# A fused transformer layer on one core: the closing norm of a mixture of experts, split into all tokens and the tokens of the last two experts

## The chip, the core and the metric

The kernel runs on one core of a Trainium2 chip. The metric is the device time of the whole kernel in microseconds (us). The engines are named as in the profile: PE is TensorE's matmuls, PEld its weight loads, DVE is VectorE, ACT is ScalarE, POOL is GpSimd, SP is SyncE; a q behind a name is the sequencer, which issues DMAs.

## The reference

One layer on 512 tokens of width 1024, in float32: a mixer of two attentions, then a mixture of experts, each followed by a residual and a LayerNorm. The change touches the end of the second half alone, so only that is shown.

```python
def layer_norm(x, g, b):
    xf = x.astype(jnp.float32)
    mu = jnp.mean(xf, axis=-1, keepdims=True)
    var = jnp.mean(jnp.square(xf - mu), axis=-1, keepdims=True)
    return ((xf - mu) * lax.rsqrt(var + LN_EPS)).astype(x.dtype) * g + b

# grouped_top2_moe: 16 experts, each token takes 2 of them
    for e in range(N_EXPERTS):
        hdn = jax.nn.silu(x2d @ w_gate[e]) * (x2d @ w_up[e])
        out = out + combine[:, e:e + 1] * (hdn @ w_down[e])

# reference
        ffn = grouped_top2_moe(x, w_router, b_router, w_gate[l], w_up[l], w_down[l])
        x = layer_norm(ALPHA * x + ffn, ln2_g[l], ln2_b[l])
```

## The kernel before

The experts are computed one after the other. An expert's tokens are gathered into slots (128 slots, or 64 from expert 10 on, `SMALL`); the token number of each slot stands in `idx`. The weights come as 512 KB loads, issued by SP in the order of use into a large ring of buffers (`big()`, `prefetch`), as early as a buffer is free. Experts from the fourth on are taken in the order of their token counts, so that 14 and 15, the last two, have the fewest tokens.

Each expert makes two products: gate and up (`pg`, eight steps c, from the lines under `if few:`), then, after `silu`, a transpose (`hidden_small`) and the second product (`down_small`, in `pu`). The second product of expert e - 1 stands inside expert e's steps, at c == 4 (`AHEAD`). Up to expert 13, POOL adds the result to the rows of `x1d` in DRAM, which holds the residual stream, by an indirect DMA (`scatter`).

The last two experts have no scatter. Their results stay on the chip: the 64 slots of expert 14 are put in partitions 0 to 63 and those of expert 15 in 64 to 127 of one pair of tiles (`split_y`: high and low parts). `final_loads`, at c == 3 of expert 15, loads the four 128-token tiles of `x1d` (`base`). A matrix `sel` of zeros and ones says which slot belongs to which token; `combine` multiplies it with the results on TensorE, so that each of the four tiles of tokens gets its sums, which DVE adds to `base` (`norm_add`). Then come mean, squares, power and the two closing multiplications, in 512-wide halves spread over DVE, ACT and POOL in an order that is written out by hand, and eight stores of 128 x 512 to the output.

In this part of the kernel every instruction goes through `ko`, which keeps the written order on each engine; an engine takes its instructions in that order and waits at the first that isn't ready. Two groups of `busy` matmuls (`WARM3`, `WARM4`) stand around the last transpose.

## Time and profile before

| | |
|---|---|
| median of 3 runs | 701.64 us (701.2 to 702.09) |
| the profiled execution's own time | 701.37 us |
| its span, first to last instruction | 699.6 us |
| busy: PE, PEld, DVE, ACT, POOL | 95%, 70%, 62%, 51%, 17% of the span |
| granted TensorE clock, mean | 0.989 |
| DMA | 155.35 MB, mean 222 GB/s |

Busy time is that of instructions of the program; a matmul's end is modelled, so that a busy PE isn't PE at its peak. The granted clock is a share of 2.4 GHz. A DMA share of 1.00 means that all 16 DMA engines of the core were taken. The idle time in brackets is that of the engine just before the instruction, with what ended it.

### The profile page before, as it was taken

The page shows a single profiled execution, that of the slowest core. Times are in us where ns is not written, and L with a number is a line of the kernel's source. Part 1 is how long each engine was busy: PE and PEld are TensorE (multiplying, and loading weights), DVE is VectorE, ACT ScalarE, POOL GpSimd, SP SyncE. Part 2 cuts the span into 40 slices and gives each one's busy share as a digit, 9 for nine tenths or more (in the row PEclk, how much of TensorE's full clock was granted, in tenths as well). Part 3 has the DMA queues.
Part 4 walks back from the last instruction along what each step waited for, and adds up shares of the span by engine and source line. Part 5 has one row for each costly group of instructions (what it writes and reads, how often), then busy time and mean ns, then how long its engine had stood idle before and what let it go on. Part 6 is the DMA issues. An engine that isn't in the chain of part 4 may idle for free.

```text
span 699.6 us, 9694 instructions
## 1 busy us (share of the span) xinstructions
PE 664.3 (95%) x3254; PEld 488.9 (70%) x3254; DVE 436.8 (62%) x740; ACT 354.0 (51%) x574; POOL 119.4 (17%) x189
## 2 busy tenths in 40 slices
PE   8999999999999999999999888999999999999970
PEld 5888778777787678888888766888888886533220
DVE  5343666667767337252545999999999998222246
ACT  5433585786656424232221236888888886211133
POOL 2000333232332110000000010111111112112016
PEclk9999999999999999999999999999999999999995
DMA  7422222211211193226993859999999999999953
GB/s 287 164 91 90 91 94 87 67 56 60 77 45 61 60 322 104 90 91 232 363 364 121 309 198 339 357 383 379 368 365 372 336 351 371 323 339 353 384 216 120
DMA packets 47062, 155.35 MB, mean 222 GB/s; under 512 B 7471, under 2 KB 7471, under 8 KB 47010
## 3 DMA queue, kind: packets, MB, share of 16 engines
q1 hardware_dynamic: 40848, 142.62, 55.8%
q0 software_dynamic: 3536, 7.82, 4.6%
q10 hardware_dynamic: 2626, 4.27, 1.8%
q8 instruction: 26, 0.43, 0.3%
q14 instruction: 26, 0.21, 0.1%
HBM read 146.87 MB, written 12.58 MB: 228 GB/s over the span
## 4 chain that ended last, share of the span: by engine, by line
PE 77%; DMA 7%; DVE 6%; issue 3%; ACT 3%; POOL 2%; DVEq 0%; POOLq 0%; SPq 0%; ACTq 0%
PE pj L149 6%; PE pj L150 5%; PE pj L151 5%; DMA raw<-in_wu_dram 5%; PE a L150 4%; PE a L151 4%; PE a L149 4%; PE py L149 3%; PE py L151 3%; PE py L150 3%; PE pg L149 2%; PE pg L1214 2%; PE pu L151 2%; PE pg L151 2%; PE pu L150 2%
## 5 line engine op out<-in xcount | busy, mean ns | idle before, releaser
L131 DVE TENSOR_TENSOR wlo<-raw,whi 128x1024 fp32r<-128x1024 f32 x169 | 202.4, 1222 | 109.2 <-ACT whi L124 105.3
L124 ACT ACTIVATE whi<-raw 128x1024 fp32r<-128x1024 f32 x169 | 174.7, 1057 | 103.8 <-issue 27.0
L149 PE MATMUL pj<-xhi,whi 128*128 128x512 f32 x192 | 81.8, 426 | 0.0
L151 PE MATMUL pj<-xhi,wlo 128*128 128x512 f32 x192 | 75.8, 395 | 0.0
L150 PE MATMUL pj<-xlo,whi 128*128 128x512 f32 x192 | 75.6, 394 | 0.0
L1041 POOL DMA_INDIRECT x1d<-y,idx x14 | 21.6, 1545 | 148.2 <-ACT y L1036 76.4
L1214 PE MATMUL pg<-raw,gh 128*64 128x512 f32 x192 | 46.1, 599 | 0.6 <-DMA raw<-in_wu_dram 0.4
L151 PEld LDWEIGHTS pj<-xhi,wlo 128*128 128x128 f32 x192 | 36.1, 188 | 8.5
L149 PEld LDWEIGHTS pj<-xhi,whi 128*128 128x128 f32 x192 | 36.6, 191 | 4.3 <-issue 0.2
L150 PEld LDWEIGHTS pj<-xlo,whi 128*128 128x128 f32 x192 | 36.4, 190 | 4.2
L312 POOL TENSOR_TENSOR p<-bt,g 128x127 f32<-128x127 f32 (+3 forms) x32 | 25.7, 812 | 52.6 <-DVE g L309 40.1
L298 POOL TENSOR_SCALAR p<-p,st 128x128 f32<-128x128 f32 (+3 forms) x32 | 17.1, 535 | 97.5 <-DVE st L297 97.5
L149 PE MATMUL py<-whi,hh 128*128 128x512 f32 x80 | 33.1, 414 | 0.0
L151 PE MATMUL py<-whi,hl 128*128 128x512 f32 x80 | 31.5, 394 | 0.0
L150 PE MATMUL py<-wlo,hh 128*128 128x512 f32 x80 | 31.5, 394 | 0.0
L309 DVE TENSOR_TENSOR_SCAN g<-l 128x128 f32<-128x128 f32 (+3 forms) x32 | 26.1, 834 | 8.4 <-ACT l L305 6.0
L1214 PEld LDWEIGHTS pg<-raw,gh 128*64 128x64 f32 x192 | 14.2, 136 | 23.7 <-issue 19.8
L893 POOL DMA_INDIRECT xg<-x1k,idx x15 | 20.5, 1370 | 58.6 <-PE pg L151 20.0
L149 PE MATMUL pg<-whi,gh 128*128 128x512 f32 x72 | 30.2, 420 | 0.0
L151 PE MATMUL pu<-whi,gl 128*128 128x512 f32 x72 | 28.5, 396 | 0.0
L151 PE MATMUL pg<-whi,gl 128*128 128x512 f32 x72 | 28.4, 395 | 0.0
L150 PE MATMUL pu<-wlo,gh 128*128 128x512 f32 x72 | 28.4, 394 | 0.0
(290 smaller groups left out, 1415.1 us busy)
## 6 DMA issues: line engine op xcount, KB each, us to landing
raw<-in_wd_dram SPq DMA_DIRECT2D x64, 512.0 KB
raw<-in_wg_dram SPq DMA_DIRECT2D x63, 512.0 KB
raw<-in_wu_dram SPq DMA_DIRECT2D x63, 512.0 KB
raw<-in_wq_dram SPq DMA_DIRECT2D x32, 512.0 KB
raw<-in_wout_dram SPq DMA_DIRECT2D x8, 512.0 KB
raw<-in_wv_dram SPq DMA_DIRECT2D x7, 512.0 KB
bt<-in_relr_dram SPq DMA_DIRECT2D x8, 256.0 KB
raw<-in_wupa_dram SPq DMA_DIRECT2D x4, 512.0 KB
```

Of the source, the lines that this page charges most:

```text
L124: ko(nc.scalar.activation(hi, raw, AF.Copy))
L131: ko(e.tensor_tensor(lo, raw, hi.bitcast(F32), op=OP.subtract))
L149: ko(nc.tensor.matmul(o, ahi, bhi, start=start, stop=False))
L150: ko(nc.tensor.matmul(o, ahi, blo, start=False, stop=False))
L151: ko(nc.tensor.matmul(o, alo, bhi, start=False, stop=stop))
L298: nc.gpsimd.tensor_scalar(p[:, :n], p[:, :n], st[:, 2, i:i + 1], 1.0, op0=OP.mult, op1=OP.mult)
L309: nc.vector.tensor_tensor_scan(g[:, :n][:, ::-1], kp[:, :n][:, ::-1], kp[:, :n][:, ::-1], 1.0, op0=OP.mult, op1=OP.bypass)
L312: nc.gpsimd.tensor_tensor(p[:, :n - 1], bt[:, :n - 1], g[:, 1:n], op=OP.mult)
L893: ko(nc.gpsimd.indirect_dma_start(out=xgb[e % NXG][:m], out_offset=None, in_=x1k, in_offset=bass.IndirectOffsetOnAxis(ap=idx[:m, e:e + 1], ...
L1041: ko(nc.gpsimd.indirect_dma_start(out=x1d, out_offset=bass.IndirectOffsetOnAxis(ap=idx[:m, e:e + 1], axis=0), in_=y[:m], in_offset=None, b ...
L1214: ko(nc.tensor.matmul(pgu[0][o], xgt[e][:, kt], w[:, ws], start=kt == 0, stop=kt == KT - 1))
```

## The change

All four tiles of tokens are normed as they stand in `x1d` without the last two experts. For the tokens that do have a slot with expert 14 or 15 this is not the result; these are normed a second time by slot, and their rows are written over the first ones.

- `final_loads` takes six loads in the order base 0, base 1, gain, base 2, base 3, offset, into buffers of another ring (`spare`); the gain and offset rows of the norm were loaded after the last product before.
- `pair_rows` gathers by indirect DMA the `x1d` rows of the 128 slots of experts 14 and 15 (`ids`).
- `same_tokens` makes a 128 x 128 matrix that is 1 where two slots hold the same token, by one matmul of ones with a diagonal of the token numbers. A token may have a slot with both experts; `same` adds up its two results in both slots.
- `copy_last` copies the two results into `ylast`, once, in plain fp32. TensorE forms pair rows plus `same` times `ylast` in `pz`.
- Tiles 0 and 1 have their statistics from DVE (`stats_v`), tiles 2 and 3 from ACT (`sum_a`, `square_a`).
- Tile 0 is finished by DVE. For tiles 1, 2 and 3 TensorE makes the output: the identity times the offset row (`offset_pe`) plus a diagonal of the inverse deviations times the centred and gained tile (`finish_pe`), both in fp32; ACT copies it out.
- The pair rows are normed by DVE from `pz`, and an indirect DMA of POOL writes them to the output.

```diff
-    off4 = const.tile([P, NT], F32, name="off4")
-    nc.gpsimd.iota(off4, pattern=[[-P, NT]], base=1, channel_multiplier=0,
...
-    def split_y(e, py, hf, part):
-        ws = slice(hf * 512, (hf + 1) * 512)
-        es = slice(0, HS) if e == NE - 2 else slice(HS, P)
-        o = py[hf * HS:(hf + 1) * HS]
-        if part == 0:
-            ko(nc.scalar.activation(yhl[0][es, ws], o, AF.Copy))
-            return
-        ko(nc.vector.tensor_tensor(yhl[1][es, ws], o, yhl[0][es, ws].bitcast(F32), op=OP.subtract))
...
-    def final_select():
-        sel = big(F32R)[:, :S]
-        gid = ep.tile([P, NT + 1], F32, name="gid")
-        ko(nc.vector.tensor_copy(gid[:HS, NT:], idx[:HS, NE - 2:NE - 1]))
-        ko(nc.vector.tensor_copy(gid[HS:, NT:], idx[HS:, NE - 1:]))
-        ko(nc.vector.tensor_scalar(gid[:, :NT], off4, gid[:, NT:], None, op0=OP.add))
-        for i in range(NT):
-            ko(nc.vector.tensor_scalar(sel[:, i * P:(i + 1) * P], slots, gid[:, i:i + 1], None, op0=OP.is_equal))
-        return sel
+    def spare(name, dt=F32):
+        return ring.tile([P, D], dt, name=name, bufs=RING)
...
+    halves = [slice(0, 512), slice(512, D)]
     def final_loads():
-        for i in range(NT):
-            base.append(big())
-            nc.sync.dma_start(base[i], x1d[i * P:(i + 1) * P])
-        lnw2.extend(big() for _ in range(2))
+        base.extend(spare(("whi", "wlo")[i // 2]) for i in range(NT))
+        lnw2.extend(spare("whi") for _ in range(2))
+        for k in (0, 1, "g", 2, 3, "b"):
+            if k in ("g", "b"):
+                t, src = (lnw2[0], ln2g) if k == "g" else (lnw2[1], ln2b)
+                ko(nc.sync.dma_start(t, src.to_broadcast([P, D])))
+            else:
+                ko(nc.sync.dma_start(base[k], x1d[k * P:(k + 1) * P]))
+    def pair_rows():
+        ids = pair["ids"] = ep.tile([P, 1], I32, name="ids")
+        ko(nc.vector.tensor_copy(ids[:HS], idx[:HS, NE - 2:NE - 1]))
+        ko(nc.vector.tensor_copy(ids[HS:], idx[HS:, NE - 1:]))
+        so = pair["sum"] = big()
+        ko(nc.gpsimd.indirect_dma_start(
+            out=so, out_offset=None, in_=x1d, in_offset=bass.IndirectOffsetOnAxis(ap=ids, axis=0),
+            bounds_check=S - 1, oob_is_err=False))
+    def same_tokens():
+        gid = ep.tile([P, 1], F32, name="gid")
+        ko(nc.vector.tensor_copy(gid, pair["ids"]))
+        diag = spare("wlo")[:, :P]
+        ko(nc.vector.tensor_scalar(diag, ident, gid, None, op0=OP.mult))
+        rows = eps_.tile([P, P], F32, name="py0")
+        onesf = ep.tile([P, 512], F32, name="gl0")[:, :P]
+        nc.gpsimd.memset(onesf, 1.0)
+        ko(nc.tensor.matmul(rows, onesf, diag, start=True, stop=True))
+        same = spare("wlo")[:, :P]
+        ko(nc.vector.tensor_scalar(same, rows, gid, None, op0=OP.is_equal))
+        return same
+    def copy_last(e, py):
+        es = slice(0, HS) if e == NE - 2 else slice(HS, P)
+        ko(nc.scalar.activation(ylast[es, :512], py[:HS], AF.Copy))
+        ko(nc.vector.tensor_copy(ylast[es, 512:], py[HS:]))
...
-                    yhl.extend(big(F32R) for _ in range(2))
-                    for hf in range(2):
-                        for part in range(2):
-                            split_y(e - 1, py, hf, part)
+                    ylast = big()
+                    copy_last(e - 1, py)
...
-            if last and c == 1:
-                sel = final_select()
...
+                pair_rows()
+                same = same_tokens()
...
+    def stats_v(i, src):
+        st = ep.tile([P, 2, 6], F32, name="st")
+        for hf in range(2):
+            ko(nc.vector.bn_stats(st[:, hf], src[hf]))
+        ko(nc.vector.bn_aggr(mv[:, i, 0:2], st.rearrange("p a b -> p (a b)")))
+    def dev_v(i):
+        ko(nc.gpsimd.tensor_scalar(mv[:, i, 1:2], mv[:, i, 1:2], EPS / ALPHA ** 2, 1.0, op0=OP.add, op1=OP.mult))
+        ko(nc.gpsimd.tensor_tensor(mv[:, i, 2:3], mv[:, i, 1:2], mhalf, op=OP.pow))
+    def sum_a(i):
+        ko(nc.scalar.activation(junk, base[i], AF.Copy, accum_out=mv[:, i, 3:4]))
+        ko(nc.gpsimd.tensor_scalar(mv[:, i, 4:5], mv[:, i, 3:4], -1.0 / D, 1.0, op0=OP.mult, op1=OP.mult))
+        ko(nc.gpsimd.tensor_scalar(mv[:, i, 0:1], mv[:, i, 3:4], 1.0 / D, 1.0, op0=OP.mult, op1=OP.mult))
+    def square_a(i):
+        ko(nc.scalar.activation(junk, base[i], AF.Square, bias=mv[:, i, 4:5], accum_out=mv[:, i, 5:6]))
+        ko(nc.gpsimd.tensor_scalar(mv[:, i, 1:2], mv[:, i, 5:6], 1.0 / D, EPS / ALPHA ** 2, op0=OP.mult, op1=OP.add))
+        ko(nc.gpsimd.tensor_tensor(mv[:, i, 2:3], mv[:, i, 1:2], mhalf, op=OP.pow))
+    def gain(i, o, src, w=slice(0, D)):
+        ko(nc.vector.scalar_tensor_tensor(o, src, mv[:, i, 0:1], lnw2[0][:, w], op0=OP.subtract, op1=OP.mult))
+    def diag_dev(i):
+        ko(nc.vector.tensor_scalar(dg[:, i * P:(i + 1) * P], ident, mv[:, i, 2:3], None, op0=OP.mult))
+    po2 = {}
+    def offset_pe(i):
+        for hf in range(2):
+            name = {1: ("pg", "pg"), 2: ("th", "tx"), 3: ("pu", "pu")}[i][hf]
+            po2[i, hf] = eps_.tile([P, 512], F32, name=name, **({"bufs": 2} if name in ("pg", "pu") else {}))
+            ko(nc.tensor.matmul(po2[i, hf], ident, lnw2[1][:, halves[hf]], start=True, stop=False))
+    def finish_pe(i):
+        for hf in range(2):
+            ko(nc.tensor.matmul(po2[i, hf], dg[:, i * P:(i + 1) * P], base[i][:, halves[hf]], start=False, stop=True))
+        for hf in range(2):
+            ko(nc.scalar.activation(xo[i][:, halves[hf]], po2[i, hf], AF.Copy))
+            ko(nc.sync.dma_start(out[i * P:(i + 1) * P, halves[hf]], xo[i][:, halves[hf]]))
+    def finish_v(i, o, w):
+        ko(nc.vector.scalar_tensor_tensor(o, o, mv[:, i, 2:3], lnw2[1][:, w], op0=OP.mult, op1=OP.add))
...
+    pyl = down_small(NE - 1, *hid)
+    stats_v(0, [base[0][:, v] for v in halves])
+    dev_v(0)
+    sum_a(2)
+    copy_last(NE - 1, pyl)
+    pz = []
+    for hf in range(2):
+        pz.append(eps_.tile([P, 512], F32, name=f"py{hf}"))
+        ko(nc.tensor.matmul(pz[hf], ident, pair["sum"][:, halves[hf]], start=True, stop=False))
+    for hf in range(2):
+        ko(nc.tensor.matmul(pz[hf], same, ylast[:, halves[hf]], start=False, stop=True))
+    xo = {i: big() for i in (1, 2, 3)}
+    stats_v(1, [base[1][:, v] for v in halves])
+    dev_v(1)
+    square_a(2)
+    sum_a(3)
+    offset_pe(1)
+    gain(0, base[0], base[0])
+    gain(1, base[1], base[1])
+    diag_dev(1)
+    finish_pe(1)
+    square_a(3)
+    stats_v(NT, pz)
+    dev_v(NT)
+    offset_pe(2)
+    gain(2, base[2], base[2])
+    diag_dev(2)
+    finish_pe(2)
+    offset_pe(3)
+    gain(3, base[3], base[3])
+    diag_dev(3)
+    finish_pe(3)
+    for w in halves:
+        finish_v(0, base[0][:, w], w)
+        ko(nc.sync.dma_start(out[:P, w], base[0][:, w]))
+    zo = pair["sum"]
+    for hf, w in enumerate(halves):
+        gain(NT, zo[:, w], pz[hf], w)
+    for w in halves:
+        finish_v(NT, zo[:, w], w)
+    ko(nc.gpsimd.indirect_dma_start(
+        out=out, out_offset=bass.IndirectOffsetOnAxis(ap=pair["ids"], axis=0),
+        in_=zo, in_offset=None, bounds_check=S - 1, oob_is_err=False))
```

What this does to the order on the engines is seen at three places. The first is ACT from the last expert's activation on (before). `raw_6364` is the high part of y, `raw_6345` and `raw_6347` are base 0 and base 1, `mv` the small tile of sums; in brackets are the semaphores that a row waits for, where DMAHW0 to DMAHW7 belong to SP's loads in turn.

```order
L1149 ACTIVATE hl<-th 128x128 [waits PE_49,Activation_49]
L1014 ACTIVATE raw_6364<-pu 64x512 [waits PE_49]
L1014 ACTIVATE raw_6364<-pu 64x512 [waits DVE_49]
L1315 ACTIVATE raw_6412,mv<-raw_6345,mv 128x512 [waits DMAHW1_49,DMAHW5_49,DMAHW0_49,Pool_49]
L1315 ACTIVATE raw_6413,mv<-raw_6347,mv 128x512 [waits DMAHW2_49,DMAHW6_49,DMAHW1_49,Pool_49]
L1315 ACTIVATE raw_6412,mv<-raw_6345,mv 128x512 [waits DVE_49]
L1318 ACTIVATE mv<-mv 128x1 [waits Pool_49]
L1315 ACTIVATE raw_6413,mv<-raw_6347,mv 128x512 [waits DVE_49]
```

And the same place in the change: `wlo` is base 2 (and, in the second L1306, base 3), `y` a tile that nobody reads, `gl_6386` the small tile of sums, `raw_6372` is `ylast`, `raw_6431` an output tile.

```order
L1134 ACTIVATE hl<-th 128x128 [waits DVE_49,PE_49]
L1306 ACTIVATE y,gl_6386<-wlo 128x1024 [waits DMAHW3_49,DMASW6_49,Pool_49]
L1183 ACTIVATE raw_6372<-pu 64x512 [waits PE_49]
L1312 ACTIVATE y,gl_6386<-wlo,gl_6386 128x1024 [waits Pool_49]
L1306 ACTIVATE y,gl_6386<-wlo 128x1024 [waits DMAHW4_49,Activation_49]
L1335 ACTIVATE raw_6431<-pg 128x512 [waits DMAHW6_49,PE_49]
L1335 ACTIVATE raw_6431<-pg 128x512 [waits PE_49]
L1312 ACTIVATE y,gl_6386<-wlo,gl_6386 128x1024 [waits Pool_49]
```

Between the activation of the last hidden tile (`hl`) and the copy of expert 15's result, ACT now has the sum over tile 2, which waits for a load; nothing stood between the two before.

The second place is DVE behind the last hidden tile, in the change alone (before, the subtraction for the low part and the adds of `norm_add` stood here). `whi` are base 0 and base 1, `raw_6372` is `ylast`.

```order
L1297 BN_STATS st<-whi 128x6 x2
L1298 BN_AGGR gl_6386<-st 128x2
L1184 COPY raw_6372<-pu 64x512
L1297 BN_STATS st<-whi 128x6 x2
L1298 BN_AGGR gl_6386<-st 128x2
L1317 SCALAR_TENSOR_TENSOR whi<-whi,gl_6386 128x1024 x2
L1320 TENSOR_SCALAR gl_6404<-ident,gl_6386 128x128
L1297 BN_STATS st<-py_6425 128x6
L1297 BN_STATS st<-py_6427 128x6
```

The statistics and gain of tile 1 and its diagonal stand behind DVE's copy of `ylast`, which is made after ACT's.

The third place is TensorE's end. Before, with `raw_6364` and `raw_6365` the high and low parts of y and `raw_6324` the matrix `sel`, it begins so, in float32r:

```order
L1296 MATMUL pg<-raw_6364,raw_6324 128x512 [waits Activation_49]
L1296 MATMUL pg<-raw_6365,raw_6324 128x512 [waits DVE_49]
L1296 MATMUL pu<-raw_6364,raw_6324 128x512
L1296 MATMUL pu<-raw_6365,raw_6324 128x512
L1296 MATMUL pg<-raw_6364,raw_6324 128x512
L1296 MATMUL pg<-raw_6365,raw_6324 128x512
L1296 MATMUL pu<-raw_6364,raw_6324 128x512 [waits DVE_49]
L1296 MATMUL pu<-raw_6365,raw_6324 128x512
L1296 MATMUL th<-raw_6364,raw_6324 128x512 [waits PE_49,Activation_49]
L1296 MATMUL th<-raw_6365,raw_6324 128x512
```

In the change it reads as follows, all in fp32; `py` are the two halves of `pz`, `raw_6372` is `ylast`, the `wlo` of the first row is `same`, `whi` with `ident` the offset row, `gl_6404` the diagonals.

```order
L1356 MATMUL py_6427<-raw_6372,wlo 128x512 [waits DVE_49]
L1329 MATMUL pg<-whi,ident 128x512 [waits DMAHW5_49]
L1329 MATMUL pg<-whi,ident 128x512
L1333 MATMUL pg<-whi,gl_6404 128x512 [waits DVE_49]
L1333 MATMUL pg<-whi,gl_6404 128x512
L1329 MATMUL th<-whi,ident 128x512 [waits PE_49]
L1329 MATMUL tx<-whi,ident 128x512 [waits PE_49]
L1333 MATMUL th<-wlo,gl_6404 128x512 [waits DVE_49]
L1333 MATMUL tx<-wlo,gl_6404 128x512
L1329 MATMUL pu<-whi,ident 128x512 x2
L1333 MATMUL pu<-wlo,gl_6404 128x512 [waits DVE_49]
L1333 MATMUL pu<-wlo,gl_6404 128x512
```

The sixteen matmuls that distributed the sums are gone; ten of the new ones stand behind the first wait for a diagonal (`gl_6404`). The last rows of POOL are

```order
L1313 TENSOR_SCALAR gl_6386<-gl_6386 128x1 [waits Activation_49]
L1314 TENSOR_TENSOR gl_6386<-gl_6386,mhalf 128x1 [waits Pool_49]
L1301 TENSOR_SCALAR gl_6386<-gl_6386 128x1 [waits DVE_49]
L1302 TENSOR_TENSOR gl_6386<-gl_6386,mhalf 128x1 [waits Pool_49]
L1386 DMA out_dram<-raw_6349,ids 512x1024 [waits DMAHW3_49,DMAHW2_49,DMAHW4_49,DMAHW1_49,DMAHW5_49,DMAHW0_49,DMAHW6_49,DMASW7_49,DMAHW7_49,DMASW0_49,DVE_49]
```

so that its scatter of the pair rows waits for all eight stores as well as for DVE; before, POOL ended with an addition.

## Rows read from the trace of the kernel before

**Rows 1.** Busy time by stage: stretch in us from the span's start, its length, then busy us (and instructions) of PE, PEld, DVE, ACT and POOL, the granted clock, the share of the DMA engines and GB/s.

```profile
600.00:620.00 20.00, 19.94 (x108) 8.73 (x108) 4.15 (x14) 3.92 (x8) 4.17 (x4) 1.00 0.98 340
660.00:670.00 10.00, 8.81 (x35) 2.31 (x32) 2.22 (x4) 2.06 (x4) 0.00 (x0) 1.00 1.01 404
670.00:680.00 10.00, 8.14 (x33) 3.86 (x32) 5.32 (x16) 3.80 (x9) 1.04 (x5) 1.00 0.45 161
680.00:690.00 10.00, 0.00 (x0) 0.00 (x0) 8.12 (x11) 6.59 (x17) 8.98 (x13) 0.71 0.14 51
690.00:699.60 9.60, 0.00 (x0) 0.00 (x0) 4.81 (x4) 0.00 (x0) 4.75 (x6) 0.50 0.44 166
```

**Rows 2.** The chain of work that ended last, in order of time: start in us, us, what.

```profile
654.40 11.20 DMA raw<-in_wu_dram
665.64 1.95 PE pg L1214 x6
670.03 3.61 PE pu L1054 x16
```

**Rows 3.** SP's issues of the four x1d loads in the timeline (start, us from the first issue to the end of the last), and, of SP's waits, what held them: us in total, times, longest.

```profile
661.87 4.12 SPq L1169 DMA_DIRECT2D raw<-x1d  x4
SPq L1169 <- DMA raw<-in_wu_dram: 1.7, 2, 0.9
```

**Rows 4.** Busy time by stage, as Rows 1, in slices of one us, where the x1d loads end and at the end of the span.

```profile
674.00:675.00 1.00, 0.49 (x1) 0.19 (x1) 0.68 (x1) 0.25 (x1) 0.00 (x0) 1.00 0.13 53
675.00:676.00 1.00, 0.98 (x4) 0.83 (x5) 0.50 (x3) 0.59 (x1) 0.00 (x0) 1.00 0.01 4
696.00:697.00 1.00, 0.00 (x0) 0.00 (x0) 0.23 (x1) 0.00 (x0) 0.00 (x0) 0.50 1.01 379
697.00:698.00 1.00, 0.00 (x0) 0.00 (x0) 0.00 (x0) 0.00 (x0) 0.00 (x0) 0.50 0.96 377
698.00:699.00 1.00, 0.00 (x0) 0.00 (x0) 0.00 (x0) 0.00 (x0) 0.00 (x0) 0.50 0.02 4
```

**Rows 5.** The timeline of DVE and POOL in the tail: start, us, engine, line, operation, out<-in and shapes.

```profile
681.92 1.28 DVE L1322 SCALAR_TENSOR_TENSOR raw<-raw,mv,raw 128x1024 f32<-128x1024 f32 x1
682.27 1.37 POOL L1328 TENSOR_TENSOR mv<-mv,mhalf 128x1 f32<-128x1 f32 x1
684.48 0.57 POOL L1328 TENSOR_TENSOR mv<-mv,mhalf 128x1 f32<-128x1 f32 x1
693.83 2.40 DVE L1338 SCALAR_TENSOR_TENSOR raw<-raw,mv,raw 128x512 f32<-128x512 f32 x2 [0.85 <-POOL mv L1328]
```

**Rows 6.** Indirect DMAs: expert 13's scatter in the timeline, then the least, median and longest time to landing of all scatters (L1041); expert 1's gather in the timeline, then its own time to landing; last the busy time, as Rows 1, of a slice just after its issue.

```profile
651.08 1.43 POOL L1041 DMA_INDIRECT x1d<-y,idx  x1 [10.21 <-DVE y L1060]
DMA to landing us min/median/max: 7.3/9.0/10.4
410.70 1.39 POOL L893 DMA_INDIRECT xg<-x1k,idx  x1 [10.92 <-DVE rank L953]
DMA to landing us min/median/max: 4.6/4.6/4.6
411.00:412.00 1.00, 1.00 (x6) 0.82 (x5) 0.93 (x4) 0.00 (x0) 1.00 (x1) 1.00 0.00 0
```

**Rows 7.** Groups of instructions by line and shape: engine, operation, names, shapes and count, then busy us in all, mean ns of one, and idle time before them.

```profile
L124 ACT ACTIVATE whi<-raw 128x1024 fp32r<-128x1024 f32 x169 | 174.7, 1057 | 103.8 <-issue 27.0 <-PE pj L150 19.4 <-PE o L151 13.1
L1059 ACT ACTIVATE y<-pu 64x512 f32<-64x512 f32 x4 | 2.4, 591 | 15.9 <-DMA x1d<-y,idx 9.5 <-PE pu L1054 6.4
L1315 ACT ACTIVATION_READ_ACCUMULATOR raw<-raw,mv 128x1 f32 x8 | 1.5, 186 | 0.0
L1060 DVE COPY y<-pu 64x512 f32<-64x512 f32 x4 | 2.8, 692 | 16.6 <-ACT y L1059 16.6
L612 DVE BATCH_NORM_STATS2 lnst<-raw 128x6 f32<-128x512 f32 x8 | 5.3, 688 | 0.1
L662 DVE BATCH_NORM_AGGREGATE lnmv<-lnst 128x2 f32<-128x12 f32 x4 | 0.8, 209 | 0.1
L682 DVE SCALAR_TENSOR_TENSOR raw<-raw,lnmv,lnw 128x1024 f32<-128x1024 f32 x3 | 3.8, 1278 | 0.0
L1163 DVE TENSOR_SCALAR raw<-slots,gid 128x128 fp32r<-128x128 f32 x4 | 0.9, 282 | 0.0
```

**Rows 8.** TensorE: eight fp32 matmuls of 128 columns (`pick`, L826) in the timeline, and their durations in ns (least, median, longest); the second product of expert 15 in the timeline, and the durations of such matmuls.

```profile
398.54 1.06 PE L826 MATMUL o<-g,raw 128*128 128x128 f32 x8
L826 PE MATMUL o<-g,raw x64: 271/275/356, 394.9 to 406.1; 128*128 128x128 f32 x64
669.96 3.65 PE L1054 MATMUL pu<-raw,hl 128*64 128x512 f32 x16
L1054 PE MATMUL pu<-raw,hl x32: 592/592/644, 656.7 to 673.0; 128*64 128x512 f32 x32
```

**Rows 9.** TensorE's clock: a matmul after a long idle stretch in the timeline, and the busy time, as Rows 1, of a slice in that stretch and of two after the last matmul.

```profile
398.05 0.66 PE L644 MATMUL a<-ident,raw 128*128 128x128 f32 x4 [2.13 <-DVE raw L611]
396.00:397.00 1.00, 0.00 (x0) 0.00 (x0) 1.00 (x2) 0.00 (x0) 0.00 (x0) 1.00 0.79 283
683.00:684.00 1.00, 0.00 (x0) 0.00 (x0) 0.81 (x3) 0.33 (x1) 0.91 (x2) 1.00 0.03 8
684.00:685.00 1.00, 0.00 (x0) 0.00 (x0) 0.00 (x0) 1.00 (x3) 0.82 (x3) 0.57 0.00 0
```

## Prediction before the run

> **What bounds the kernel now.** I read the busy share by stage first, then the chain of work that ended last, then the timeline of the last 40 us engine by engine. Up to 670 us the 16 DMA engines are at 0.98 to 1.04 of their time [rows 1]: the weight stream sets the pace, and the chain runs through loads of wd and wu until 665.6 us [rows 2]. From there the end is a string of dependent steps: the last matmuls of expert 15's first product, its activation, its second product (matmuls until 673.6), then 26 us of norm work on ACT, DVE and POOL. Between 680 and 699.6 TensorE does nothing at all [rows 1]. The change rewrites this tail only; up to the last expert's c == 3 each engine has the same instructions in the same order, but for one small constant that goes.
>
> Two facts of the tail matter. First, SP issues the four x1d loads from 661.87 on, 1.26 us apart, each when the weight load eight places ahead is complete [rows 3]; they queue behind the last weights, and DMA traffic ends only in the slice 674:675 (0.13, then 0.01) [rows 4]. So the fourth load in SP's line is complete at about 675.4, later than the last matmul of expert 15 (673.6). Before, that cost nothing, since the fourth tile was added late. Second, after the last DVE instruction (ends 696.23: it begins at 693.83 with two in 2.40, [rows 5]) there are 3.35 us to the span's end: one store, whose traffic fills the slice 697:698 and is over in 698:699 [rows 4], and the end of the program.
>
> **The change part by part.** *Removed*: the eight splits of y, the sixteen combine matmuls, eight adds, squares in halves, POOL's half-tile adds. *Added ahead of 673.6*: diag, one 128x128 matmul and `same`, on engines that wait for weights then (TensorE is held by raw loads until 665.6 [rows 2]); nothing. The gather of the 128 pair rows is not free. The reference's inputs give the last two experts 44 and 43 tokens, so 87 rows of 4 KB, 0.36 MB, come in between. It waits for expert 13's scatter, issued at 651.08, which lands 7.3 to 10.4 us later [rows 6], so it enters a full DMA at about 661 and pushes what is behind it back. At 0.512 MB in 1.26 us [rows 3] that is 0.9 us spread evenly and 1.26 us where an engine has all of its share; nothing if it meets engines that are ahead. I take 1.1, bounds 0 and 1.3. It delays the last wu load (to 666.7 at most), so expert 15's second product ends near 674.7.
>
> *The new order on ACT* is what I rest on. `sum_a(2)` stands ahead of `copy_last`, and base[2] is now the fourth load in SP's line, since the gain row goes ahead of it. So ACT waits until 675.4 + 1.1 = 676.5, although y is ready at 674.7. Behind ACT's copy stand DVE's copy and everything that DVE does after it. The steps, from [rows 7]:
> - `sum_a(2)`, 1024 elements: 1.06 as an activation of this size, 0.19 for reading the accumulator: 677.8
> - ACT's copy 0.59, DVE's copy 0.69: 679.1
> - `stats_v(1)`: two BN_STATS of 0.69 and 0.21 to aggregate, 1.6: 680.7
> - `gain(0)` and `gain(1)`, 128x1024 each as L682, 2 x 1.28: 683.2
> - POOL's add and power for tile 1 are small, but one power took 1.37 instead of 0.57 while DVE ran a 1.28 us instruction, and ended 0.44 behind it [rows 5]: 683.65. Bounds: already done (0), or both after (0.85)
> - `diag_dev(1)` 0.28: 683.95
>
> *TensorE's outputs.* From there TensorE has ten matmuls in a row with nothing to pull them forward: finish 1, offset 2, finish 2, offset 3, finish 3, two halves each. Plain fp32 on the full array stands in no row at 512 columns. Each fp32 matmul shows as two records: 32 picks gave 64 [rows 8]. At 128 columns eight records took 1.06 us, the last one 0.275 of it, so a record every 0.112, and a pick 0.224; four times the columns give 0.86. The second product gives the same: 16 records in 3.65 us, two at a time in the two column halves, so 0.43 a record [rows 8]. Ten take 8.6: 692.55, and 0.16 until the last sum can be read (a record of that product lasts 0.59, not 0.43): 692.7. The other tiles' diagonals are no later: DVE after diag 1 has the pair's statistics 1.6, gain 2 and diag 2 1.56 (687.1; TensorE wants it at 687.4), gain 3 1.28 and diag 3 behind ACT's square of tile 3 and POOL (about 689.2; wanted at 690.8). ACT copies the last half until 693.3 and SP stores it.
>
> *The last scatter.* POOL's scatter of the pair rows writes the same tensor as the eight stores, so it waits until all have landed. A store and the program's end together took 3.35; the scatter goes in between. DVE's pair rows (six halves behind diag 3, 0.7 each as the 512-wide rows of [rows 7]) are done by about 693.4, two us before the stores, and cost nothing. An indirect DMA on otherwise idle queues: issued at 410.70, DMA share 0.00 in 411:412, landed 4.6 us after the start [rows 6]; 54 rows there by the same inputs, 87 here. Under load it took 7.3 or more, which does not apply with the weights gone. I take 4.6 and 0.2 for the waits ahead of it; lower bound 3.2 (the instruction's 1.39 and a store's 1.8 us of traffic).
>
> Sum: 693.3 + 3.35 + 4.8 = 701.45 against a span of 699.56: 1.9 us more. The profiled execution took 701.37, 0.27 less than the median of 701.64; on the median, 703.5.
>
> The Trainium skill, "DMA: Bandwidth & Descriptors", section "Anatomy of one DMA — SWDGE (gpsimd) path", has a fit for such a DMA: some 2.0 us fixed and the bytes at 436 GB/s. For 0.36 MB that estimate is 2.8 us, and by it the sum would be 701.5. The row says 4.6 for fewer bytes, with POOL's instruction alone at 1.39, so this trace does not agree and the sum keeps the row.
>
> **The rivals.** All are against 701.64; 0.2% of it, 1.4 us, is about what a measurement of this kernel can tell from no change.
> - *The last scatter costs little more than a store* (not slower). The place is the end, the price 3.2 instead of 4.6 and 0.2: 701.9. For it: the destination is plain and no queue is busy. Against it: [rows 6]. It decides from 4.3 us down: then the time is within 0.2%. The fit cited above would have it so.
> - *The fourth load isn't late* (not slower): the gather hits other engines than the laggards, or its rows are absorbed. Then the chain starts at 675.4 and the sum falls by 1.1: 702.4. If the load even came before 674.7 it would be 701.7. Against it: the traffic's end at 675 [rows 4] is measured, and nothing was taken out ahead of it.
> - *Several bounds at their low end*, the two above together and POOL hidden: 1.6 + 1.1 + 0.65 less, 700.1, just faster. This is the only road to a gain that I see: 26 us of tail before, and after it a chain that has the load, ten matmuls, a store and a scatter one behind the other.
> - *TensorE's clock falls* (slower still). It stands idle twice in my chain: from about 676.4 to 678.4 (waiting for y) and 682.0 to 684.0 (for diag 1). An idle stretch of 2.13 us at 396 left the granted clock at 1.00; after the last matmuls before 680 it was at 1.00 in 683:684 and 0.57 in 684:685, that is, it went from 2.4 to 1.2 GHz some 4.5 us after the work ended [rows 9]. So it should hold. If it falls ahead of the ten matmuls they cost up to 17.2 instead of 8.6: between 705 and 712 with a partial recovery. The Trainium skill, "TensorE: Matmul & The Clock Gate", section "Why this matters for your kernels", warns of idle gaps between bursts of matmuls for this reason; the trace shows no gap of this size that did it.
>
> **How the numbers follow.** The forecast's own case, 702.3 to 705, 0.54; scatter cheap or load in time, 701 to 703, 0.26; low ends together, 0.12; clock, 0.08. Faster by over 0.2% is the low ends' case and a little: 0.12. Within 0.2% are the two middle rivals and the lower edge of the forecast (703.04 is the limit): 0.31. Slower: 0.57. The likeliest is 703.5, its own range 702.3 to 705. For 8 in 10 I go from 700.0 (the low ends) to 706.0 (the clock's first step), with about 0.1 on either side. Cases of both signs are in it, but the forecast's own holds more than half.
>
> **What would show it.** Right: ACT idle before `sum_a(2)` until about 676.5 with a DMA as what ended it; DVE's second copy after 678; TensorE busy without a gap for 8 to 9 us until about 692.6 at a clock of 1.00; POOL's last DMA issued around 695.6 and the span ending more than 5 us later. Wrong: `sum_a(2)` starting right after expert 15's activation (the load was in time); the ten matmuls at other than 0.86 each; diag 1 well before 683.5; the span ending less than 4.5 us after POOL's last issue; any stage before 655 moved.

## The result

The changed kernel takes 708.25 us (median of ten runs, 705.12 to 710.69), the kernel before, run beside it, 703.3 us (ten runs, 700.16 to 707.33): a ratio of 1.0069 with an interval of 1.0047 to 1.009, some 4.9 us slower. The forecast was 703.5 and 1.9 us slower; its direction was right, its size was less than half, and 708.25 lies above its range. 1.7 us of the distance come from the kernel before, whose median was 701.64 in three runs and 703.3 in ten, so from here on only differences are compared. In a later comparison one of the changed kernel's seven executions took 3807 us; it is left out of the ratio.

The chain of work that ended last, in the profile of the changed kernel (start in us, us, what):

```profile
660.24 11.92 DMA raw<-in_wu_dram
...
672.22 10.12 DMA wlo<-x1d
...
682.44 1.15 ACT y L1306 x2
...
683.61 0.60 ACT raw L1183
...
684.23 0.71 DVE raw L1184
...
684.96 1.30 DVE st L1297 x2
...
687.77 1.49 POOL gl L1302
...
689.28 0.30 DVE gl L1320
...
689.62 1.98 PE pg L1333 x4
...
696.76 1.73 PE pu L1333 x4
...
698.51 0.61 ACT raw L1335
...
700.06 2.47 DMA out_dram<-whi
...
703.32 1.33 POOLq L1432
```

It is the chain that the forecast wrote down: last weights, fourth x1d load (`wlo`, tile 2), ACT's sum, the two copies, statistics of tile 1, gains, POOL's power, diagonal 1, TensorE's matmuls, ACT's copy, store, POOL. Where it departs from the forecast is at its two ends. The last wu load is issued at 660.24, and at 654.40 before [rows 2]: the changed kernel comes to its tail 5.8 us late. And the end behind ACT's last copy is longer than forecast. It reads so in the timeline, with the time from issue to landing (us) from the list of DMA issues in the last row:

```profile
691.41 8.06 SPq L1336 DMA_DIRECT2D out_dram<-raw  x6
699.56 0.90 SPq L1380 DMA_DIRECT2D out_dram<-whi  x2
703.56 1.10 POOL L1386 DMA_INDIRECT out_dram<-raw,ids  x1 [7.02 <-issue]
out_dram<-raw,ids POOLq DMA_INDIRECT x1, 3.3
```

Tile 0's two stores (L1380) stand behind the other six on SP. The last of them is issued at 700.06 and lands at 702.53; the scatter starts at 703.56 and lands 3.3 us later, at 706.9; the span ends at 709.05. By stage (columns as [rows 1]):

```profile
670.00:680.00 10.00, 9.26 (x38) 2.47 (x35) 2.43 (x5) 0.87 (x2) 0.00 (x0) 1.00 0.98 391
680.00:690.00 10.00, 6.17 (x15) 2.41 (x14) 5.32 (x9) 4.13 (x7) 4.27 (x8) 1.00 0.10 39
690.00:700.00 10.00, 8.47 (x20) 3.42 (x18) 8.09 (x13) 4.71 (x8) 3.40 (x7) 1.00 0.36 132
700.00:709.20 9.20, 0.00 (x0) 0.00 (x0) 0.00 (x0) 0.00 (x0) 1.10 (x1) 0.69 0.32 123
```

TensorE's clock is at 1.00 through its matmuls, and in the last nine microseconds nothing is computed: there are stores, one scatter and waits.

### The profile page after: what moved, and what is told of

The parts are those of the page before. It is cut to its first block, busy times and chain, and to the rows that moved or that the text cites. A ratio compares the mean times of both kernels' runs of the same rounds, so it can differ in the third digit from the quotient of the medians.

```text
span 709.1 us, 9702 instructions
## 1 busy us (share of the span) xinstructions
PE 680.9 (96%) x3272; PEld 495.1 (70%) x3272; DVE 433.0 (61%) x731; ACT 351.9 (50%) x563; POOL 113.5 (16%) x182
```

## The experiments

They were set against two theories. T: all of the loss is in the tail, and the 5.8 us ahead of it are chance of one execution. E: the changed program is late ahead of the tail, too. S and P are about the start, where TensorE's clock rises from 1.2 to 2.4 GHz at different times: by S that is chance, by P it comes later where a program ends with an indirect scatter. A, B and C belong to the constant, below. All numbers of the runs stand in this table; "landing" is the last wu load's, worked out from the row of that load (issue and length), "to end" is from there to the end of the span. The kernel without the gather ran once, so that it has no ratio; only its profile is used.

| kernel | wu load issued | lands after | to end | ratio to before |
|---|---|---|---|---|
| before | 654.40 | 11.20 | 34.0 | |
| before, again | 655.60 | 11.22 | 34.0 | 0.9985 (0.996 to 1.001) |
| changed | 660.24 | 11.92 | 36.9 | 1.0069 (1.0047 to 1.009) |
| changed, again | 658.96 | 11.90 | 36.9 | 1.0093 (1.0059 to 1.0128) |
| changed, third | 656.97 | 11.92 | 36.9 | 1.009 (1.0068 to 1.0111) |
| no scatter | 654.79 | 11.94 | 31.4 | 1.0005 (0.9979 to 1.003) |
| plain store | 656.33 | 11.88 | 34.2 | 1.003 (1.0006 to 1.0055) |
| sum behind copy | 656.87 | 11.88 | 34.0 | 1.0042 (1.0017 to 1.0068) |
| tile 0 stored first | 657.41 | 11.89 | 35.5 | 1.0072 (1.0053 to 1.0091) |
| no gather | 658.42 | 11.19 | 36.9 | |
| constant back | 656.37 | 11.87 | 36.8 | 1.0025 (1.0001 to 1.0048) |
| constant back, 2 | 654.67 | 12.17 | 37.0 | 1.0056 (1.0032 to 1.0079) |
| before, padded | 656.25 | 11.19 | 33.9 | 1.0014 (0.9994 to 1.0035) |
| before, shifted | 659.41 | 10.78 | 33.9 | 1.0037 (1.0016 to 1.0057) |
| before, shifted, 2 | 657.66 | 11.20 | 33.9 | 1.0025 (1.0004 to 1.0045) |
| best | 659.94 | 11.92 | 32.1 | 0.9971 (0.9949 to 0.9993) |

**The two kernels once more.** No edit.

> The kernel before once more, to see how far two executions of one program lie apart. Theory T (the tail alone differs): from the landing of the last wu load to the end of the span 33.9 us again (33.5 to 34.3), whatever the rest does, and the issue of the last wd load anywhere between 658 and 667 us, so that the 5.9 us by which the changed kernel's profile was late there are the execution's and not the program's. Rival E (the changed kernel is late early, too): the last wd load at 660.6 within 1 us, as in the first profile. Ratio to the kernel before 1.000 by both.

> The changed kernel once more. Theory T: from the landing of the last wu load to the end 36.9 us (36.5 to 37.4), 3.0 more than before, and with 0.7 for the gather ahead of it 3.7 us in all: a ratio near 1.005. Rival E: the last wd load is issued at 665 or later again, 4 us or more behind the repeated kernel before, and the ratio is 1.007 or more.

The tail is as fixed as theory T has it: 34.0 and 36.9 us in every profile of the two, so with the gather's 0.7 ahead (shown below) the tail accounts for 3.6 us. But the changed kernel was late again ahead of it (last wd load at 665.19, 3.3 us behind the repeated kernel before, whose own stood at 661.85, not at 660.6; E had asked for 4) and its ratio, 1.0093, was E's. T was right on the tail and wrong in "all".

**The scatter at the end.** First it is left out, then a plain store takes its place:

```
-    ko(nc.gpsimd.indirect_dma_start(out=out, out_offset=..., in_=zo, ...))
+    ko(nc.sync.dma_start(out[:P], zo))          # second kernel only
```

> The changed kernel without its last scatter: the rows of the pair are normed but not written to the output. Theory T, from the changed kernel's profile: the end follows the landing of tile 0's last plain store by 1.05 us, so from the landing of the last wu load to the end 31.4 us, 5.5 less than with the scatter, and the kernel is 1.8 us faster than before (ratio 0.9975). By the price in the forecast (4.6 and 0.2 for waits) it would be 4.8 less: 32.1 us, ratio 0.9985. If the scatter is hidden beside other work of the program's end: less than 2 us.

> The changed kernel with one plain store by SP in place of the last scatter: the 128 normed rows of the pair go to the first 128 rows of the output, where they don't belong, behind the same wait for tile 0's stores. Theory T: the 0.8 us between POOL's last wait and its DMA, the 3.3 us to landing and the 1.3 us of POOL's drain behind the landing belong to an indirect DMA; a plain store of 512 KB lands some 2.5 us after its issue and the end follows 1.05 us later: from the last wu load's landing to the end 34.2 us, 2.7 less than with the scatter. Rival: any DMA that is issued last costs this, so only 0.9 us of the landing is saved: 36.0 us.

31.4 and 34.2 us to the end: both as the profile of the changed kernel had it. The scatter costs 5.5 us, not 4.8; a plain store of the same bytes in the same place costs 2.7. The difference lies on both sides of the transfer. In the trace POOL's last wait ends at 702.77 and the DMA starts at 703.56; it lands at 706.90, but POOL's closing drain (a DRAIN instruction at the end of its program) is over at 708.21 only, and the program's end of 0.84 us comes behind that. In all nine profiles with this scatter the drain ends 1.27 to 1.31 us behind the landing. Before, POOL's drain was over at 697.48, 1.0 us ahead of the landing of SP's last store (698.46), and the span ended 1.1 us behind that landing.

**SP's order, and ACT's.** Tile 0's rows and stores move ahead of `finish_pe(3)`; in the other kernel the sum moves behind the copy:

```
+    for w in halves: finish_v(0, ...); store of tile 0
     finish_pe(3)
-    for w in halves: finish_v(0, ...); store of tile 0
```
```
-    sum_a(2)
     copy_last(NE - 1, pyl)
+    sum_a(2)
```

> The changed kernel with tile 0's two stores issued ahead of tile 3's two on SP; DVE's order is the same. Theory T: SP's last store ahead of the scatter is issued when ACT's last copy ends, not 0.93 us later, so the whole end moves up by 0.9: 36.0 us from the last wu load's landing to the end. Rival: tile 0's rows are late and hold SP, or the landings queue on the DMA engines all the same: 36.7 or more. The clock at the start as in the run with the later sum: theory S anywhere from 4.8 to 10.5, rival P at 10.4.

> The changed kernel with ACT's sum over tile 2 moved behind its copy of expert 15's product, so that nothing ahead of the copy waits for the fourth load. Theory T: the copy starts when the second product ends, DVE's copy is done some 9.3 us after the last wu load has landed instead of 12.8, and diag 1 follows; then the sixth load (ln2b) bounds TensorE's ten matmuls, which end 3.2 us earlier: from the last wu load's landing to the end 33.7 us instead of 36.9, and a ratio to before of 1.001 by the tail alone. Rival: the diagonals of tiles 2 and 3 or another load are late next and less than 2 us is saved (35 us or more). On the start, theory S (which of the clock's rises an execution gets is chance): the granted clock reaches 1.00 anywhere from 4.8 to 10.5 us; rival P (a program that ends with an indirect scatter starts the next execution with a later rise): at 10.4 again, as in both profiles of the changed kernel.

With tile 0 stored first 1.4 us are saved, not 0.9. The chain's row of the last store is

```profile
696.27 2.01 DMA out_dram<-raw
```

against 700.06 and 2.47 above: it is issued as ACT's copy ends (0.93 earlier), and alone it lands 0.46 sooner than as the third of three. With the sum later 2.9 us are saved, of 3.2 expected. The timeline of ACT, TensorE and DVE there:

```profile
676.81 0.59 ACT L1183 ACTIVATE raw<-pu 64x512 f32<-64x512 f32 x1 [3.85 <-PE pu L1039]
679.05 1.06 ACT L1306 ACTIVATE y<-wlo 128x1024 f32<-128x1024 f32 x1 [1.65 <-DMA wlo<-x1d]
681.50 1.98 PE L1329 MATMUL pg<-whi,ident 128*128 128x512 f32 x4 [1.10 <-DMA whi<-in_ln2b_dram]
683.02 0.29 DVE L1320 TENSOR_SCALAR gl<-ident,gl 128x128 f32<-128x128 f32 x1 [0.99 <-POOL gl L1302]
```

ACT's copy now waits for TensorE, not for the load; the sum waits for the load, where nobody stands behind it. Diagonal 1 is begun 14.3 us after the last wu load has landed (668.75) instead of 17.1. What holds TensorE now is the sixth load, ln2b, for the offset of tile 1. So the order on ACT, on which the forecast rested, did cost about what it said (1.8 us of load and 1.25 of sum, 3.05 in all, against the 2.9 that came back). The granted clock rose to 1.00 at 4.9 us with tile 0 first and at 10.8 us with the sum later, though both end with the scatter: rival P has fallen.

**The gather.** The tile is filled with zeros by POOL instead:

> The changed kernel without the gather of the pair's 128 rows: POOL fills the tile with zeros, so the pair's rows lack their earlier sum. Theory T: the last wu load lands 11.25 us after its issue as in the kernel before (11.24 there, 11.9 in every profile with the gather); the rest of the tail stays at 36.9. By the forecast the gather costs 1.1, so 10.8; if it costs nothing, 11.9 stays and the 0.7 is something else. The clock at the start: theory S anywhere from 4.8 to 10.5, rival P at 10.4 (it still ends with the scatter).

```profile
658.42 11.19 DMA raw<-in_wu_dram
```

The load lands 11.19 us after its issue, 0.7 less than with the gather: theory T. The forecast had 1.1. This is one profile, but the table bears it out: without the gather the load lands after 10.78 to 11.22 us, with it after 11.87 to 12.17.

**The constant.** All profiles of the changed kernel and of those made from it so far lose about one microsecond more between 36 and 340 us, where the program is the same. There TensorE is busy for 302 of 304 us, and it is its own matmuls that take longer. Busy time of the matmuls into `pj`, then into `a`, from 12 to 345 us (columns as [rows 1] but for POOL): two rows for each of the kernel before, the changed one, the changed one with the constant back, and the kernel before, shifted.

```profile
12.00:345.00 333.00, 156.19 (x576) 102.01 (x576) 33.00 (x48) 32.88 (x56) 1.00 0.34 117
12.00:345.00 333.00, 89.80 (x384) 72.27 (x384) 10.94 (x16) 4.64 (x8) 1.00 0.34 117
```
```profile
12.00:345.00 333.00, 156.87 (x576) 102.06 (x576) 33.00 (x48) 32.85 (x56) 1.00 0.33 113
12.00:345.00 333.00, 90.50 (x384) 72.24 (x384) 10.94 (x16) 4.64 (x8) 1.00 0.33 113
```
```profile
12.00:345.00 333.00, 156.24 (x576) 102.01 (x576) 33.02 (x48) 32.89 (x56) 1.00 0.34 117
12.00:345.00 333.00, 89.80 (x384) 72.25 (x384) 10.94 (x16) 4.64 (x8) 1.00 0.34 117
```
```profile
12.00:345.00 333.00, 156.88 (x576) 102.08 (x576) 33.02 (x48) 32.85 (x56) 1.00 0.33 114
12.00:345.00 333.00, 90.50 (x384) 72.25 (x384) 10.94 (x16) 4.63 (x8) 1.00 0.33 114
```

With the change, 960 matmuls take 1.4 us longer. What changed for them is where their operands stand: `off4`, 16 bytes a partition, is gone, and all tiles allocated behind it, the split weights `whi` and `wlo` first, stand 32 bytes earlier (the first `whi` at byte 19264 of a partition instead of 19296). Three kernels test that:

```
+    off4 = const.tile([P, NT], F32, name="off4")          # constant back, in the changed kernel
+    nc.gpsimd.iota(off4, ...)
```
```
+    pad = const.tile([P, NT], F32, name="pad")             # before, padded: 32 bytes later
+    nc.gpsimd.memset(pad, 0.0)
```
```
-    off4 = const.tile([P, NT], F32, name="off4")           # before, shifted: 32 bytes earlier
+        off4 = ep.tile([P, NT], F32, name="off4")          # in final_select, at the end
```

> The changed kernel with the small constant off4 (16 bytes a partition, filled by one POOL instruction at the start, read by nothing) put back, so that all tiles behind it in SBUF, the split weights whi and wlo first, stand 32 bytes further on, where they stand in the kernel before. In all seven profiles of the changed kernel and its variants TensorE's matmuls of 512 columns in the projections take longer than in both profiles of the kernel before, by one or two ns each: the three groups of pj 82.1, 76.0 and 75.9 us against 81.8, 75.8 and 75.6, and a<-olo,whi 25.5 against 25.3. Theory A (the address does it): the groups are back at 81.8, 75.8, 75.6 and 25.3, and of what the start to 340 us loses 1 us comes back; the tail stays at 36.9 us from the last wu load's landing; ratio to before 1.0055 (3.7 us of 702). Rival: the durations have to do with something else in the program: they stay at 82.1 and the rest, ratio 1.007.

> The kernel before with one more constant of 16 bytes a partition, set to zero at the start by POOL and read by nothing, so that whi, wlo and what follows stand 32 bytes further on than in the kernel before and 64 further on than in the changed one. Theory A: the address alone slows the projections: pj at 82.1, 76.0 and 75.9 us as in the changed kernel if what counts is the address by 64 bytes; the end of the program is the same 33.9 us from the last wu load's landing; ratio 1.001 to 1.002. Rival: only the changed program's own code does it, 81.8, 75.8, 75.6, ratio 1.000.

> The changed kernel a third time, on the same chip as the next run, to price the 32 bytes in time. Theory A (3.7 us of tail and 1.1 us of slower projections): ratio to before 1.007, pj at 82.1, 76.0 and 75.9 us, 36.9 us from the last wu load's landing to the end. Rival (there is a third part, of 1 us or more, in how often the clock falls at 400 to 420 us): ratio 1.009 again.

> The changed kernel with the constant put back, once more. Theory A: 1.1 us below the changed kernel beside it (0.16%), ratio to before 1.0055, pj at 81.8, 75.8 and 75.6 us. Rival (the 32 bytes cost more than TensorE's groups show): 3 us or more below the changed kernel, ratio 1.0025 again as in the first such run.

> The kernel before with the constant off4 made at the end, in the pool of the experts' small tiles, and not at the start: whi, wlo and all tiles behind them then stand 32 bytes earlier, where they stand in the changed kernel; all engines have the same instructions in the same order but for this one of POOL, which POOL has time for. The tail and the gather of the changed kernel are not in it. Theory A (32 bytes cost what TensorE's groups show, 1.1 us): pj at 82.1, 76.0 and 75.9 us, ratio 1.0016. Rival B (they cost all of the 3.1 us by which the changed kernel stood above its twin with the constant, medians of 22 and 24 runs): ratio 1.0045. Rival C (the address is not it): pj at 81.8, 75.8 and 75.6, ratio 1.000.

> The same kernel a second time, for a second profile and twice the runs: as in the first, theory A 1.0016, rival B 1.0045, rival C 1.000; and whether TensorE's clock falls between 395 and 425 us, as in nine of eleven profiles whose addresses differ from the kernel before and in none of its two: theory A takes that for chance.

The rows above decide: with the constant back the durations are those of the kernel before; the kernel before, with its addresses shifted and one POOL instruction moved to the end, has those of the changed one. That it is the address and not this instruction is seen in the padded kernel, which has the instruction at the start and other addresses (19328): its two rows have 156.77 and 90.14, 0.9 us more than the kernel before. In time the shift alone costs 0.37% and 0.25%, 2.2 us on the mean, between theory A's 1.1 and rival B's 3.1; each interval reaches from the one to the other, so which is nearer stays open, but the rival by which the address is not it has fallen. Padded the other way it costs 0.14%, 1.0 us, which is about what its rows show but lies within the error of nothing. In the changed kernel a constant that nobody reads is worth about 2 us.

1.4 of the 2.2 are in the rows. The rest may be TensorE's clock, which falls in 12 of all 16 profiles between 395 and 425 us (below): in 8 of 10 with the shifted addresses, in 3 of 5 without, and in the padded one (the count in the last expectation had taken in kernels whose addresses are those of before): too few to say that the shift brings it about. That is left open.

With the 2.2 us the other ratios come out, too. The difference of "to end" to 34.0, 0.7 for the gather and 2.2 for the shift, over 702 us, give, as an estimate, 1.0004 without the scatter, 1.0044 with the plain store, 1.0041 with the sum later and 1.0063 with tile 0 first; 1.0005, 1.003, 1.0042 and 1.0072 were measured, each interval taking in its estimate. By theory T alone the kernel without the scatter should have been at 0.9975, faster than before. Of the two runs with the constant back, where the 2.2 are left out (1.0050), one interval ends just below (1.0048) and the other takes it in.

**A kernel with all of it.** It computes everything. ln2b is loaded first, ACT copies before it sums, TensorE takes in the pair's earlier sum and all offsets while it would wait, the diagonals come before tile 0's rows, tile 0 is stored ahead of tile 3, and the constant is back:

```
-        for k in (0, 1, "g", 2, 3, "b"):
+        for k in ("b", 0, 1, "g", 2, 3):
...
     offset_pe(1); stats_v(0, ...); dev_v(0)
     copy_last(NE - 1, pyl)
...
     sum_a(2); ...; sum_a(3); square_a(2); square_a(3)
     gain(1, ...); diag_dev(1); offset_pe(2); finish_pe(1); offset_pe(3)
     gain(2, ...); gain(3, ...); diag_dev(2); finish_pe(2); diag_dev(3)
     gain(0, ...); tile 0's rows and stores; stats_v(NT, pz); dev_v(NT); finish_pe(3)
```

> All that was learned in one kernel, which computes everything: off4 back; the loads in the order ln2b, tiles 0 and 1, ln2g, tiles 2 and 3; TensorE takes the pair's earlier sum in while it waits for the last hidden tile, the offsets of tile 1 behind the second product and those of 2 and 3 before tile 1 is finished; ACT copies expert 15's product before its sums; DVE makes the diagonals before tile 0's rows, whose stores go ahead of tile 3's; the statistics of the pair last. Worked out from the profile of the run with the later sum: TensorE's last matmul 20.6 us after the last wu load has landed instead of 23.5, DVE's last row 23.4, the scatter's wait over some 0.3 us behind, and 6.3 us from there to the end: 30.9 us against 33.9 before, with 0.7 for the gather 2.3 us faster than before, ratio 0.997. Rival: DVE, which has the pair's rows last, or the loads bound it and the end stays above 33.2: no faster than before.

0.9971 (0.9949 to 0.9993): 2 us faster than before, where 2.3 were expected. But the tail is 32.1 us, not 30.9: by it and the gather 1.2 us would be saved, which the interval takes in as well. Three pieces of its chain, then SP and POOL at the end:

```profile
673.16 10.16 DMA wlo<-x1d
...
688.51 1.28 DVE wlo L1320
...
689.80 0.21 DVE gl L1323
```
```profile
693.12 0.91 SPq L1379 DMA_DIRECT2D out_dram<-whi  x2
694.12 0.99 SPq L1339 DMA_DIRECT2D out_dram<-raw  x2
698.49 1.10 POOL L1388 DMA_INDIRECT out_dram<-raw,ids  x1 [2.57 <-DVE raw L1342]
```

TensorE ends 21.9 us after the last wu load's landing, not 20.6. With ln2b ahead tile 2's load is complete 11.5 us after that landing (683.32), not 10.2; ACT's sums and squares follow it, then the gain of tile 3, and only behind that stands diagonal 2. Tile 0's second half comes out of DVE at 693.4 and holds tile 3's first store a little. The scatter at the end still costs what it did.

## Why the prediction was wrong in size

Moved by the 5.84 us between the issues of the last wu load, its steps can be laid beside the profile:

| step | forecast + 5.84 | measured |
|---|---|---|
| fourth load complete | 682.3 | 682.3 |
| ACT's sum done | 683.6 | 683.6 |
| both copies | 684.9 | 684.9 |
| statistics of tile 1 | 686.5 | 686.5 |
| two gains | 689.0 | 688.8 |
| POOL's power | 689.5 | 689.3 |
| diagonal 1 | 689.8 | 689.6 |
| last matmul | 698.4 | 698.5 |
| ACT's last copy | 699.1 | 699.1 |
| end of the span | 707.3 | 709.05 |

- **The chain** held to 0.3 us over 17 us: that the fourth load would hold ACT, that DVE's second copy and all behind it would follow, POOL's late power (1.49 here, 1.37 in [rows 5]) and ten matmuls at 0.86, as worked out from the 16 records of the second product [rows 8] (the other way to it was a slip: four times the 0.224 of a pick are 0.90). In one place two errors cancel: the gather costs 0.7, not 1.1, and the fourth load is complete 10.2 us after the last wu load, 0.4 later than I read from the traffic's end [rows 4].
- **The last scatter** is the first step that failed: from ACT's last copy to the end 8.15 us in the sum, 9.9 measured. Three of its terms were missing or wrong. "One store", 2.25 us of the 3.35 up to its landing, were three, since tile 0's two stand behind it on SP (0.93 to their issue, 0.46 more to land): 3.4 us. "0.2 for the waits ahead" were 1.0 from the landing to the DMA's start. And "the program's end", taken over from a kernel that ended with SP's store, is 2.2 us behind the indirect DMA's landing instead of 1.1 behind a store's, because POOL's drain comes in between. Against that the scatter itself took 3.3 us, not the 4.6 of [rows 6]. Together this is 1.8 us. The rival that the scatter is cheap was right on the transfer (3.3 for its 3.2) and wrong on what that would bring.
- **"But for one small constant that goes"**, priced at nothing, is the second: 2.2 us by the shifted kernel before. I asked what the instruction cost and not where the tiles behind it would stand. The sign "any stage before 655 moved" came: 1.4 us of this are in the matmuls of the projections.
- **The sum** with both mended: 34.0 to 36.9 us of tail, 0.7 of gather, 2.2 of shift, 5.8 us; the three comparisons of the changed kernel gave 4.9, 6.5 and 6.3.
- **The clock in the tail**: in two of the changed kernel's three profiles it fell to 0.50 for 3.4 us (from 682.8 and 681.1), as TensorE waited for y and took it in, and was back before the ten matmuls; the tail was 36.9 us with it and without. That rival's price did not come about. But my argument against it, "so it should hold", rested on one execution: where the clock stayed at 1.00 in the kernel before, behind the gap of 2.13 us [rows 9], it falls in both profiles with the constant back (at 397.8 and 398.0). The Trainium skill, "TensorE: Matmul & The Clock Gate", section "Why this matters for your kernels", names idle gaps between bursts of matmuls as the reason for a fall. Two of the three profiles agree, with a fall around the end of a wait of 2.2 us; the first profile has the same wait and keeps 1.00.
- **The price by a fit.** The Trainium skill, "DMA: Bandwidth & Descriptors", section "Anatomy of one DMA — SWDGE (gpsimd) path", gives an estimate of 2.8 us. The transfer took 3.3, nearer to it than my row. POOL's 0.8 us ahead of the transfer and 1.3 behind it were measured on top of that.

## What to carry to other kernels

A DMA of another kind at the end of a program brings its own end with it: price it from its last wait to the span's end, with all that stands ahead of it on the issuing queue, and not by its transfer alone. When an allocation goes, look up which operands move, and compare the durations of untouched matmuls in the two profiles before explaining the time by the part that was changed. A wait that is put ahead of a copy on an in-order engine costs all that stands behind the copy; here moving one line gave back 2.9 us.

## What the hardware showed that was not expected

- Operands 32 bytes earlier in SBUF make matmuls of 512 columns longer by 1.2 ns (`pj`, 0.68 us over 576) and 1.8 ns (`a`, 0.70 over 384); 32 bytes later than in the kernel before they are longer as well (0.58 and 0.34 us; the 64 of `a<-olo,whi` take 25.5 us instead of 25.3). Why these addresses differ the runs don't show.
- POOL's drain ended 1.3 us after the landing of its own indirect DMA, to within 0.05 us in nine profiles.
- TensorE's clock can fall in one execution and not in another at the same place. In the kernel before TensorE is idle for 1.54 us at 413.8 to 415.3, then has twelve tiny matmuls until 416.0, and the clock stays at 1.00 (first row, of the kernel before). In the changed kernel, 3.2 us later and with 1.51 us of idle time, it falls (the other rows):

```profile
400.00:430.00 30.00, 25.20 (x152) 17.85 (x152) 28.31 (x71) 13.12 (x17) 3.69 (x3) 1.00 0.72 244
```
```profile
400.00:430.00 30.00, 25.85 (x150) 18.45 (x150) 26.88 (x73) 12.86 (x17) 3.70 (x3) 0.94 0.68 232
420.00:421.00 1.00, 1.00 (x2) 0.34 (x1) 0.97 (x4) 0.00 (x0) 0.00 (x0) 0.55 0.72 291
421.00:422.00 1.00, 1.00 (x3) 0.24 (x2) 1.00 (x3) 0.00 (x0) 0.70 (x1) 0.50 0.08 33
423.00:424.00 1.00, 1.00 (x3) 0.37 (x2) 0.23 (x1) 0.85 (x2) 0.09 (x1) 0.74 0.54 139
```

  The loads behind it are issued some 1.4 us later for it (the distance to the kernel before grows from 3.2 to 4.6 us). At the start the rise from 1.2 to 2.4 GHz varies likewise: a matmul of the same size at 7.5 us takes 0.40 us in the profile of the kernel before and 0.63 in the changed one's, which loses 2.0 us there; the rise came between 4.8 and 10.9 us in the sixteen profiles. Of the 5.8 us by which the changed kernel's first profile came late to its tail, these two make some 3.4 and the projections 1.4; the last microsecond, lost behind 600 us, isn't explained. In sets of ten and more, executions of one program lie 4 to 8 us apart: a single profile's early delay doesn't show by itself what a change did.

```profile
7.53 0.40 PE L151 MATMUL s<-whi,xlo 128*128 128x512 f32 x1
```
```profile
7.61 0.63 PE L146 MATMUL s<-whi,xhi 128*128 128x512 f32 x1
```
